# Turning one block of attention probabilities by two transposing transfers instead of on TensorE

## The chip, the cores and the metric

The kernel runs on one core of a Trainium2 chip. The metric is the device time of one execution in microseconds (us). The kernel before took 906.15 us, the median of three runs (905.28 to 908.67).

## What is computed

An encoder trunk of two layers on 256 tokens with 1024 features, in float32. One projection of the normalised input gives the inputs of two branches and two gates; their sum goes through an output projection, a SwiGLU block and a per-layer embedding. The reference, cut to the part around the change:

```python
def hybrid_layer(h, ...):
    u = rms_norm(h, g_mix_pre)
    (gq, gk, gv, gg, ra_f, ra_b, aq, ak, av, gate_a, gate_b) = split(u @ w_in)
    o_gla = rms_norm(o_f + o_b, g_gla_out)          # gated linear attention, both directions
    branch_a = (o_gla * silu(gg)) @ w_o_gla
    q = rope(rms_norm(aq, g_q_norm)); k = rope(rms_norm(ak, g_k_norm))
    branch_b = gqa_attention(q, k, av) @ w_o_attn   # 8 heads in 2 groups, softmax over 256 keys
    mixed = sigmoid(gate_a) * branch_a + sigmoid(gate_b) * branch_b
    h = h + rms_norm(mixed @ w_out, g_mix_post)
    ...
```

## The kernel before

**Products.** Every float32 matrix product is made of three matmuls of fp32r operands: each operand is split into a high part (a cast, on ScalarE, ACT in the profile) and a low part (source minus high part, on VectorE, DVE); both are written by `split`, L135. A block of weights of 1 MB is loaded by SyncE's queue (SP, L298), split into `wh` and `wl`, and used by 24 matmuls of 128x512, 12 for each half of the tokens (8 with `wh`, 4 with `wl`, L123). The class `Stream` holds three raw buffers and four pairs of split weights, so a load starts when a raw buffer has been split, and a split starts when TensorE (PE) is done with an older pair. `ws.cast` is the pair of instructions, cast and subtraction, of the weight split made last.

**Order.** The program is written as a main line of weight products and a set of tasks. After each product a `tick()` counts the tasks down; a task whose count is up writes its next piece and yields the next count. A scheduler then sorts each engine's instructions by that order, with a few raised in priority (`tc.high_priority`) and a few tied behind another instruction (`tc.issue_after`). The result is one fixed order for each engine; at run time an engine takes its instructions in that order and waits at any whose inputs are not there.

**The stages that matter here**, in each of the two layers, by the part of the name behind the underscore and the layer's number: `v` and `gg` (the value and out-gate projections of the gated linear attention, GLA), `gla` (its scores and its four outputs, `outputs`, L1384 on), `at0`/`at1` (the softmax attention of the two groups of heads), `gate` (the product of gate A as plain blocks, that of gate B in a form with seven products of quarter blocks instead of eight, and the product of branch A with `w_o_gla`). What runs there:

- Attention, `attend(g)`, for the two query halves `hf` of group g: scores and `softmax` (exponentials at L1237 on ACT, normalising at L1244 on DVE) give a tile of probabilities `pr_`, 128 queries by 4 heads by 256 keys. `turn_p` (L1249 on) transposes it on PE, eight 128x128 blocks into two banks of PSUM (L1254), and splits each bank (L135, tiles `mid_0at`). Then 6 matmuls of 128x512 multiply by the values (`aux_0at`), and the result is split into `aT` (`big_0at`).
- The four GLA outputs: 12 matmuls of 128x256 each, two squares with their sums on ACT (L1396), the reciprocal root on GpSimd (POOL, L494 and L495), two scalings on DVE (L544), into the tile `on`, whose index s is the half of the tokens: the outputs come for half 0 twice, then for half 1 twice.
- The out-gate, `out_gate`, starts when the GLA and the attention tasks are both over: sigmoids on ACT (L1457), eight products on DVE (L128, tiles `mid_0gg`), then `turn_out`: the 16-bit halves of the words are set apart by an ACT copy (L466) and transposed by an SP transfer (L467), four in all; later `take_in` joins them again (ACT copy, L476) and splits them into `gT` (`big_0gg`), the operand of the branch-A product `m`.
- The sums that the seven-product form of gate B needs: `whole` (four additions at L1510, two products at L128, one split) and four more additions at L131, then splits into `mid_0gate`; between the weights, additions of whole weight blocks (L327, L330, L333, in `Stream.step`).

The string `GATES` gives the order of the weight products of the gate stage: three of gate A (u), then gate B (digits) and branch A (m) interleaved.

Of the kernel before, what the change touches and what calls it, by code (L numbers as in the profile page):

```python
# [11 lines left out]
F32R = mybir.dt.float32r  # L12
BF16 = mybir.dt.bfloat16
U16 = mybir.dt.uint16
# [4 lines left out]
P = 128  # L19
# [6 lines left out]
AHEAD, EMPTY, EMPTY_FIRST = 400, 100, 1600  # L26
# [5 lines left out]
WAIT_SPREAD = 12  # L32
W = dict(r=5, z=6, s0=4, s=3, s1=9, o0=1, o=1, k=4, q=3, a0=1, a1=4, a2=4, a3=1)
WAIT_GATED = 9, 11

STEPS_FIRST = "00 10 01 11 02 12 03 13".split()
STEPS = "00 01 02 10 03 11 12 13".split()
# [24 lines left out]
def trunk_kernel(ctx: ExitStack, tc: tile.TileContext, a: dict, out: bass.AP):  # L62
# [7 lines left out]
    nc = tc.nc  # L70
# [13 lines left out]
    def nm(s):  # L84
        uid[0] += 1
        return f"{s}_{part[0]}_{uid[0]}"

    def big(dt=F32):
        return bigp.tile([P, 2048], dt, tag="big", name=nm("big"))

    def mid(dt=F32):
        return b4p.tile([P, 1024], dt, tag="mid", name=nm("mid"))
# [4 lines left out]
    def aux():  # L97
        return accp.tile([P, 512], F32, tag="acc", name=nm("aux"))
# [16 lines left out]
    def passes(o, parts, start, stop, fresh=False, between=None, **kw):  # L115

        ps = [((xh, yh), (xh, yl), (xl, yh)) if fresh else ((xh, yh), (xl, yh), (xh, yl)) for (xh, xl), (yh, yl) in parts]  # L120
        seq = [p for t in ps for p in t[:2]] + [t[2] for t in ps]
        for n, (x, y) in enumerate(seq):
            nc.tensor.matmul(o, x, y, start=start and n == 0, stop=stop and n == len(seq) - 1, **kw)  # L123
            if between is not None and 2 * (n + 1) == len(seq):
                between()
# [7 lines left out]
    def split(hi, lo, src):  # L133

        return nc.scalar.copy(hi, src), nc.vector.tensor_tensor(out=lo, in0=src, in1=hi.bitcast(F32), op=ALU.subtract)  # L135


    h = cp.tile([P, 2, D], F32, tag="h", name="h")
# [229 lines left out]
    ws = Stream(4)  # L368
# [101 lines left out]
    def take_in(hi, lo, src, parts, behind=()):  # L470

        tn = hi.shape[-1]
        with ExitStack() as order:
            for x in behind:
                order.enter_context(tc.issue_after(x.ins))
            nc.scalar.copy(  # L476
                parts.bitcast(U16).rearrange("p (k t s) -> p k t s", s=2, t=tn),
                src.bitcast(U16).rearrange("p (s k t) -> p k t s", s=2, t=tn),
            )
            split(hi, lo, parts.rearrange("p (k t) -> p k t", t=tn))  # L480
# [65 lines left out]
    def halves(t):  # L546
        return [t[:, j * 512 : (j + 1) * 512] for j in range(2)]
# [501 lines left out]
    for l in range(DEPTH):  # L1049
# [199 lines left out]
        def turn_p(pr_):  # L1249
            res = []  # L1250
            for s in range(2):
                ps = aux()
                for i in range(4):
                    nc.tensor.transpose(ps[:, i * P : (i + 1) * P], pr_[:, i, s * P : (s + 1) * P], ident)  # L1254
                pT = halves(mid(F32R))
                split(pT[0], pT[1], ps)
                res.append(pT)
            return res

        def attend(g):  # L1260
            qs = []
            for hf in range(2):
                yield W["q"]
                ps = aux()
                for i in range(4):
                    hd = 4 * g + i
                    nc.tensor.transpose(ps[:, i * P : (i + 1) * P], qrs[hf][:, hd * P : (hd + 1) * P], ident)
                qh, ql = halves(mid(F32R))
                split(qh, ql, ps)
                qs.append((qh, ql, qss[hf][:, 4 * g : 4 * g + 4]))  # L1270
            keys.need()
            yield W["a0"]
            prs = []
            for hf in range(2):
                prs.append(softmax(g, hf, qs[hf]))
                yield W["a1"]
            for hf in range(2):
                pT = turn_p(prs[hf])
                yield W["a2"]
                o = aux()  # L1280
                vs = [slice(s * 256 + g * P, s * 256 + (g + 1) * P) for s in range(2)]
                passes(o, [((avh[:, c], avl[:, c]), pT[s]) for s, c in enumerate(vs)], True, True)
                aT.put(o, 4 * g, 4, hf * P, P)
                yield W["a3"]

        def attention():
            for g_ in range(2):
                part[0] = f"{l}at{g_}"
                yield from attend(g_)
# [90 lines left out]
        on = big().rearrange("p (s c) -> p s c", s=2)  # L1380
# [70 lines left out]
        def out_gate():  # L1451
            while not (gla.over and attention.over):
                yield 1
            for hf in range(2):
# [11 lines left out]
                def turn(hf=hf, xs=xs):  # L1466
                    for j, x in enumerate(xs):
                        yield WAIT_GATED[hf] if j == 0 else 1
                        take_in(*gT.at(4 * j, 4, hf * P, P), *x)
# [322 lines left out]
```

## Time and profile before

| | before |
|---|---|
| median of 3 runs | 906.15 us |
| the profiled execution | 905.28 us, of it 903.5 us from its first to its last instruction |
| granted TensorE clock | 0.998 of full speed |
| PE busy | 894.6 us (99%), 4447 matmuls |
| DVE busy | 790.9 us (88%) |
| ACT busy | 634.5 us (70%) |
| POOL busy | 105.4 us (12%) |
| HBM read | 169.50 MB |

The times in the profile are microseconds from the start of the span. A row of the timeline gives the start, the time up to the end of the last of the row's instructions, the engine, line, operation, output tile and inputs, their shapes and how many instructions the row stands for; brackets at its end give idle time before it and what ended it. A tile `mid_0at` is one of the pool `mid`, layer 0, stage `at`. A row of the windows gives, for a stretch of time, the busy us (and number of instructions) of PE, PE's weight loads, DVE, ACT and POOL, then the clock, the share of the transfer engines and their GB/s.

### The profile page before, as it was taken

To read this page: it belongs to the slowest core of one execution; us is meant where nothing else is said; L and a number is where in the kernel's file an instruction comes from. 1 tells how busy PE (TensorE), PEld (TensorE's weight loads), DVE (VectorE), ACT (ScalarE), POOL (GpSimd) and SP (SyncE) were. 2 spreads that over 40 slices of the span, in tenths; PEclk is the share of its full clock that TensorE was granted. 3 is DMA by queue.
4 is the path that set the end of the run, shared out by engine and by line. 5 is a ranking of instruction groups with operands and counts; after the bars stand their busy time and mean duration, and the time that the engine had idled before them with its cause. 6 is when DMAs were issued, how large, how long until landed. Compare 5 with 4: busy or idle time off the path is not lost.

```text
span 903.5 us, 12157 instructions
## 1 busy us (share of the span) xinstructions
PE 894.6 (99%) x4447; PEld 759.9 (84%) x4447; DVE 790.9 (88%) x1021; ACT 634.5 (70%) x1027; POOL 105.4 (12%) x157
## 2 busy tenths in 40 slices
PE   9999999999999999999999999999999999999996
PEld 8888888878888888888898888888888888888886
DVE  7899979988569989999779799799985799999984
ACT  7678769856468787766676687698645697867653
POOL 3800111220110000000334001210001100000001
PEclk9999999999999999999999999999999999999999
DMA  8764448369296785947476424475672966857441
GB/s 285 255 200 138 140 140 236 138 231 315 66 328 192 208 266 175 291 171 265 161 268 213 160 94 140 140 232 184 218 251 91 306 187 221 255 182 261 151 176 47
DMA packets 116967, 180.25 MB, mean 200 GB/s; under 512 B 30942, under 2 KB 55014, under 8 KB 116396
## 3 DMA queue, kind: packets, MB, share of 16 engines
q1 hardware_dynamic: 116748, 179.35, 60.9%
q8 instruction: 35, 0.57, 0.3%
q14 instruction: 24, 0.20, 0.1%
q10 hardware_dynamic: 160, 0.14, 0.0%
HBM read 169.50 MB, written 3.15 MB: 191 GB/s over the span
## 4 chain that ended last, share of the span: by engine, by line
PE 86%; DVE 6%; ACT 3%; issue 3%; POOL 1%; DMA 1%; POOLq 0%; ACTq 0%; DVEq 0%
PE acc_0ffnin L123 12%; PE acc_1ffnin L123 11%; PE acc_1gate L123 7%; PE acc_1ffnin L107 7%; PE acc_0ffnin L107 7%; PE acc_1rq L123 3%; PE acc_1gqk L107 2%; PE acc_0wout L123 2%; PE acc_0ple L123 2%; PE acc_1gg L123 2%; PE acc_1v L123 2%; PE acc_0v L123 2%; PE acc_1merge L123 2%; PE acc_0merge L123 2%; PE acc_1ple L123 2%
## 5 line engine op out<-in xcount | busy, mean ns | idle before, releaser
L135 ACT CAST wh_1ffnin<-raw_1ffnin 128x1024 fp32r<-128x1024 f32 x38 | 38.7, 1051 | 20.8 <-PE acc_1ffnin L107 11.1
L135 ACT CAST wh_0ffnin<-raw_0ffnin 128x1024 fp32r<-128x1024 f32 x38 | 38.5, 1049 | 19.4 <-PE acc_0ffnin L107 9.3
L135 DVE TENSOR_TENSOR wl_0ffnin<-raw_0ffnin,wh_0ffnin 128x1024 fp32r<-128x1024 f32 x38 | 44.9, 1221 | 4.0 <-ACT wh_0ffnin L135 4.0
L135 DVE TENSOR_TENSOR wl_1ffnin<-raw_1ffnin,wh_1ffnin 128x1024 fp32r<-128x1024 f32 x38 | 45.0, 1221 | 2.8 <-ACT wh_1ffnin L135 2.7
L107 PE MATMUL acc_0ffnin<-wh_0ffnin,big_0ffnin 128*128 128x512 f32 x176 | 45.1, 390 | 0.0
L107 PE MATMUL acc_1ffnin<-wh_1ffnin,big_1ffnin 128*128 128x512 f32 x176 | 45.1, 390 | 0.0
L123 PE MATMUL acc_1ffnin<-wh_1ffnin,big_1wout 128*128 128x512 f32 x168 | 41.5, 389 | 0.0
L123 PE MATMUL acc_0ffnin<-wh_0ffnin,big_0wout 128*128 128x512 f32 x168 | 41.5, 389 | 0.0
L107 PEld LDWEIGHTS acc_0ffnin<-wh_0ffnin,big_0ffnin 128*128 128x128 f32 x176 | 33.0, 188 | 6.9
L107 PEld LDWEIGHTS acc_1ffnin<-wh_1ffnin,big_1ffnin 128*128 128x128 f32 x176 | 33.0, 188 | 6.9
L123 PEld LDWEIGHTS acc_1ffnin<-wh_1ffnin,big_1wout 128*128 128x128 f32 x168 | 31.5, 188 | 6.5
L123 PEld LDWEIGHTS acc_0ffnin<-wh_0ffnin,big_0wout 128*128 128x128 f32 x168 | 31.5, 188 | 6.5
L135 DVE TENSOR_TENSOR wl_1ffnin<-lent_1ffnin,wh_1ffnin 128x1024 fp32r<-128x1024 f32 x30 | 35.6, 1220 | 0.8 <-ACT wh_1ffnin L135 0.7
L135 DVE TENSOR_TENSOR wl_0ffnin<-lent_0ffnin,wh_0ffnin 128x1024 fp32r<-128x1024 f32 x30 | 35.7, 1220 | 0.3 <-ACT wh_0ffnin L135 0.3
L135 ACT CAST wh_1ffnin<-lent_1ffnin 128x1024 fp32r<-128x1024 f32 x30 | 30.5, 1054 | 5.4 <-PE acc_1ffnin L107 2.5
L135 ACT CAST wh_0ffnin<-lent_0ffnin 128x1024 fp32r<-128x1024 f32 x30 | 30.4, 1051 | 4.9 <-DVE wl_0ffnin L135 2.5
L135 DVE TENSOR_TENSOR wl_0gate<-raw_0gate,wh_0gate 128x1024 fp32r<-128x1024 f32 x20 | 24.7, 1265 | 3.2 <-ACT wh_0gate L135 3.1
L135 ACT CAST wh_0gate<-raw_0gate 128x1024 fp32r<-128x1024 f32 x20 | 20.2, 1055 | 7.4 <-PE acc_0gate L123 3.5
L135 DVE TENSOR_TENSOR wl_1gate<-raw_1gate,wh_1gate 128x1024 fp32r<-128x1024 f32 x20 | 23.6, 1220 | 1.6 <-ACT wh_1gate L135 1.6
L135 ACT CAST wh_1gate<-raw_1gate 128x1024 fp32r<-128x1024 f32 x20 | 20.1, 1046 | 6.4 <-PE acc_1gate L123 3.5
L107 PE MATMUL acc_1ffnin<-wl_1ffnin,big_1ffnin 128*128 128x512 f32 x88 | 24.1, 391 | 0.0
L107 PE MATMUL acc_0ffnin<-wl_0ffnin,big_0ffnin 128*128 128x512 f32 x88 | 24.0, 391 | 0.0
(730 smaller groups left out, 2745.1 us busy)
## 6 DMA issues: line engine op xcount, KB each, us to landing
raw_0ffnin<-in_w_ffn_out_dram SPq DMA_DIRECT2D x11, 1024.0 KB, 5.2
raw_1ffnin<-in_w_ffn_out_dram SPq DMA_DIRECT2D x11, 1024.0 KB, 5.9
lent_0ffnin<-in_w_ffn_in_dram SPq DMA_DIRECT2D x6, 1024.0 KB, 5.1
lent_1ffnin<-in_w_ffn_in_dram SPq DMA_DIRECT2D x6, 1024.0 KB, 6.9
raw_0v<-in_w_in_dram SPq DMA_DIRECT2D x4, 1024.0 KB, 5.2
raw_0gate<-in_w_o_gla_dram SPq DMA_DIRECT2D x4, 1024.0 KB, 5.3
raw_0gate<-in_w_o_attn_dram SPq DMA_DIRECT2D x4, 1024.0 KB
raw_0wout<-in_w_ffn_in_dram SPq DMA_DIRECT2D x8, 512.0 KB, 4.6
```

Of the source, the lines that this page charges most:

```text
L107: return nc.tensor.matmul(o, lhsT, rhs, start=start, stop=stop)
L123: nc.tensor.matmul(o, x, y, start=start and n == 0, stop=stop and n == len(seq) - 1, **kw)
L135: return nc.scalar.copy(hi, src), nc.vector.tensor_tensor(out=lo, in0=src, in1=hi.bitcast(F32), op=ALU.subtract)
```

## The change

For group 1 and the first query half, in each layer, the eight PE transposes are replaced. `turn_p_out` sets the two 16-bit planes of each half of the keys apart by an ACT copy into `on[:, 1, :]`, which is still free, and one SP transfer for each half transposes them back into the tile of the probabilities. After three more ticks `turn_p_in` joins the planes by an ACT copy into `on[:, 1, :]`, tied behind the last weight split written so far, and splits the result from there. The second query half still goes through `turn_p`.

```diff
+TURNED_P, WAIT_P = (0,), 3
...
+        def turn_p_out(pr_, hf):
+            flat, planes = pr_.rearrange("p h k -> p (h k)"), on[:, 1 - hf, :]
+            with tc.high_priority(AHEAD):
+                for s, t in enumerate(halves(planes)):
+                    nc.scalar.copy(
+                        t.bitcast(U16).rearrange("p (z h f) -> p z h f", z=2, f=P),
+                        pr_[:, :, s * P : (s + 1) * P].bitcast(U16).rearrange("p h (f z) -> p z h f", z=2),
+                    )
+            xs = list(zip(halves(flat), halves(planes)))
+            for src, t in xs:
+                nc.sync.dma_start_transpose(out=src.bitcast(U16).rearrange("p (x t) -> p x t", t=P), in_=t.bitcast(U16))
+            return xs
+
+        def turn_p_in(xs):
+            res = []
+            for src, t in xs:
+                pT = halves(mid(F32R))
+                take_in(*(x.rearrange("p (k t) -> p k t", t=P) for x in pT), src, t, ws.cast)
+                res.append(pT)
+            return res
...
             for hf in range(2):
                 prs.append(softmax(g, hf, qs[hf]))
                 yield W["a1"]
+                if g and hf in TURNED_P:
+                    prs[hf] = turn_p_out(prs[hf], hf)
             for hf in range(2):
-                pT = turn_p(prs[hf])
+                if g and hf in TURNED_P:
+                    yield WAIT_P
+                    pT = turn_p_in(prs[hf])
+                else:
+                    pT = turn_p(prs[hf])
                 yield W["a2"]
```

Lines behind the new functions move by 28 (L1510 becomes L1538), those ahead by 1. The attention task of group 1 now ends later, by which more moves than the probabilities. On PE, besides the eight transposes that go, the second half's eight transposes move from ahead of the first GLA output to behind the third, and its six value products from inside the first gate product to behind two gate products. GpSimd's order stays as it was, and SP gets the two transfers between two weight loads. Three places of the fixed order follow, of layer 0; layer 1 has the same.

The first is DVE around the last GLA outputs (`aux_0gla_..`; the scaled outputs go into `big_0gla_..929`, which is `on`). Before, from an addition of `whole` just ahead of the first output's scaling to the scaling of the third:

```order
L1510 TENSOR_TENSOR mid_0gate_250_1615<-big_start_46_303 128x512
L544 SCALAR_TENSOR_TENSOR big_0gla_136_929<-aux_0gla_237_1492,hss_0gla_238_1493,ggla_0gla_135_927 128x256 x2
L1510 TENSOR_TENSOR mid_0gate_251_1616<-big_start_22_149 128x512
L1510 TENSOR_TENSOR mid_0gate_251_1616<-big_start_46_303 128x512
L128 TENSOR_TENSOR mid_0gate_251_1616<-mid_0gate_251_1616,rope0_0kv_91_638 128x512 x2
L544 SCALAR_TENSOR_TENSOR big_0gla_136_929<-aux_0gla_239_1518,hss_0gla_240_1519,ggla_0gla_135_927 128x256 x2
L135 TENSOR_TENSOR mid_0gate_252_1623<-mid_0gate_251_1616,mid_0gate_252_1623 128x512
L131 TENSOR_TENSOR mid_0gate_251_1616<-mid_0gate_251_1616 128x512
L131 TENSOR_TENSOR t512_0gate_253_1626<-mid_0gate_250_1615,mid_0gate_251_1616 128x512
L131 TENSOR_TENSOR mid_0gate_251_1616<-mid_0gate_251_1616,mid_0gate_250_1615 128x512
L131 TENSOR_TENSOR mid_0gate_250_1615<-mid_0gate_250_1615,t512_0gate_253_1626 128x512
L544 SCALAR_TENSOR_TENSOR big_0gla_136_929<-aux_0gla_241_1544,hss_0gla_242_1545,ggla_0gla_135_927 128x256 x2
```

In the changed kernel, on DVE from the scaling of the last output on:

```order
L545 SCALAR_TENSOR_TENSOR big_0gla_136_929<-aux_0gla_241_1566,hss_0gla_242_1567,ggla_0gla_135_927 128x256 x2
L1538 TENSOR_TENSOR mid_0gate_247_1602<-big_start_22_149 128x512
L1538 TENSOR_TENSOR mid_0gate_247_1602<-big_start_46_303 128x512
L1538 TENSOR_TENSOR mid_0gate_248_1603<-big_start_22_149 128x512
L1538 TENSOR_TENSOR mid_0gate_248_1603<-big_start_46_303 128x512
L129 TENSOR_TENSOR mid_0gate_248_1603<-mid_0gate_248_1603,rope0_0kv_91_638 128x512 x2
L136 TENSOR_TENSOR mid_0gate_249_1610<-mid_0gate_248_1603,mid_0gate_249_1610 128x512
L136 TENSOR_TENSOR big_0at_234_1521<-aux_0at_253_1642,big_0at_234_1521 128x4x128
L132 TENSOR_TENSOR mid_0gate_248_1603<-mid_0gate_248_1603 128x512
L132 TENSOR_TENSOR t512_0gate_250_1613<-mid_0gate_247_1602,mid_0gate_248_1603 128x512
L132 TENSOR_TENSOR mid_0gate_248_1603<-mid_0gate_248_1603,mid_0gate_247_1602 128x512
L132 TENSOR_TENSOR mid_0gate_247_1602<-mid_0gate_247_1602,t512_0gate_250_1613 128x512
```

Before, the additions of `whole` and the sums stood between the scalings; now all of them stand behind the last scaling, behind the split `big_0at_..1521` of the second half's value product too.

The second place is DVE a few rows on: the out-gate's products (`mid_0gg`) and the splits of the weights `wl_0gate_..1665` (gate B's first), `..1722` (gate A's last) and `..1756` (gate B's second), which were `..1689`, `..1726` and `..1768`. Before, from the split of the last attention result to the first addition of weights:

```order
L135 TENSOR_TENSOR big_0at_230_1461<-aux_0at_249_1606,big_0at_230_1461 128x4x128
L128 TENSOR_TENSOR mid_0gg_254_1636<-mid_0gg_254_1636,big_0gg_201_1276 128x512 x2
L128 TENSOR_TENSOR mid_0gg_254_1636<-mid_0gg_254_1636,big_0gla_136_929 128x512 x2
L128 TENSOR_TENSOR mid_0gg_255_1646<-mid_0gg_255_1646,big_0gg_201_1276 128x512 x2
L128 TENSOR_TENSOR mid_0gg_255_1646<-mid_0gg_255_1646,big_0gla_136_929 128x512 x2
L135 TENSOR_TENSOR mid_0gate_256_1657<-mid_0gate_250_1615,mid_0gate_256_1657 128x512
L135 TENSOR_TENSOR mid_0gate_257_1666<-mid_0gate_251_1616,mid_0gate_257_1666 128x512
L135 TENSOR_TENSOR mid_0gate_258_1675<-mid_0gate_251_1616,mid_0gate_258_1675 128x512
L135 TENSOR_TENSOR wl_0gate_265_1689<-lent_0gate_259_1678,wh_0gate_264_1688 128x1024 x2
L135 TENSOR_TENSOR mid_0gate_266_1701<-t512_0gate_253_1626,mid_0gate_266_1701 128x512
L327 TENSOR_TENSOR lent_0gate_259_1678<-lent_0gate_259_1678,lent_0gate_261_1682 128x2048
```

In the changed kernel, from the split of gate B's first weights to that of its second:

```order
L136 TENSOR_TENSOR wl_0gate_261_1665<-lent_0gate_255_1654,wh_0gate_260_1664 128x1024 x2
L136 TENSOR_TENSOR mid_0gate_251_1624<-mid_0gate_247_1602,mid_0gate_251_1624 128x512
L136 TENSOR_TENSOR mid_0gate_252_1633<-mid_0gate_248_1603,mid_0gate_252_1633 128x512
L136 TENSOR_TENSOR mid_0gate_254_1651<-mid_0gate_248_1603,mid_0gate_254_1651 128x512
L328 TENSOR_TENSOR lent_0gate_255_1654<-lent_0gate_255_1654,lent_0gate_257_1658 128x2048
L129 TENSOR_TENSOR mid_0gg_262_1677<-mid_0gg_262_1677,big_0gg_201_1276 128x512 x2
L129 TENSOR_TENSOR mid_0gg_262_1677<-mid_0gg_262_1677,big_0gla_136_929 128x512 x2
L129 TENSOR_TENSOR mid_0gg_263_1687<-mid_0gg_263_1687,big_0gg_201_1276 128x512 x2
L129 TENSOR_TENSOR mid_0gg_263_1687<-mid_0gg_263_1687,big_0gla_136_929 128x512 x2
L136 TENSOR_TENSOR mid_0gate_264_1697<-t512_0gate_250_1613,mid_0gate_264_1697 128x512
L136 TENSOR_TENSOR wl_0gate_267_1722<-raw_0gate_258_1660,wh_0gate_266_1721 128x1024 x2
L136 TENSOR_TENSOR wl_0gate_272_1756<-big_0gate_256_1656,wh_0gate_271_1755 128x1024 x2
```

Before, the eight out-gate products stood ahead of the first gate-B split; now they stand behind it and behind the first addition of weights, and the split of gate A's last weights stands behind all of these.

The third place is PE, where gate A's last block uses that split (`acc_..1729` and `1730` now, `1733` and `1734` before, are its two halves of the tokens). Before:

```order
L123 MATMUL acc_0gate_279_1776<-wh_0gate_264_1688,big_start_22_149 128x512 x8
L123 MATMUL acc_0gate_279_1776<-wl_0gate_265_1689,big_start_22_149 128x512 x4
L123 MATMUL acc_0gate_271_1733<-wh_0gate_268_1725,big_start_46_303 128x512 x8
L123 MATMUL acc_0gate_271_1733<-wl_0gate_269_1726,big_start_46_303 128x512 x4
L123 MATMUL acc_0gate_272_1734<-wh_0gate_268_1725,big_start_46_303 128x512 x8
L123 MATMUL acc_0gate_272_1734<-wl_0gate_269_1726,big_start_46_303 128x512 x4
```

In the changed kernel:

```order
L124 MATMUL acc_0gate_275_1764<-wh_0gate_260_1664,big_start_22_149 128x512 x8
L124 MATMUL acc_0gate_275_1764<-wl_0gate_261_1665,big_start_22_149 128x512 x4
L124 MATMUL acc_0gate_269_1729<-wh_0gate_266_1721,big_start_46_303 128x512 x8
L124 MATMUL acc_0gate_270_1730<-wh_0gate_266_1721,big_start_46_303 128x512 x7
L124 MATMUL acc_0gate_269_1729<-wl_0gate_267_1722,big_start_46_303 128x512 x2
L124 MATMUL acc_0gate_270_1730<-wh_0gate_266_1721,big_start_46_303 128x512
L124 MATMUL acc_0gate_270_1730<-wl_0gate_267_1722,big_start_46_303 128x512 x2
```

Before, each half's matmuls with `wh` were followed by its own with `wl`; now seven of the second half's `wh` matmuls are taken ahead of the first that needs `wl_0gate_..1722`.

## The prediction

> **What bounds the kernel now.** First the page: what is busy, and the chain that ended last.
>
> ```profile
> span 903.5 us, 12157 instructions
> ...
> PE 894.6 (99%) x4447; PEld 759.9 (84%) x4447; DVE 790.9 (88%) x1021; ACT 634.5 (70%) x1027; POOL 105.4 (12%) x157
> ...
> PE 86%; DVE 6%; ACT 3%; issue 3%; POOL 1%; DMA 1%; POOLq 0%; ACTq 0%; DVEq 0%
> ```
>
> PE is the bound. Next, what PE waits for in the whole span:
>
> ```profile
> PE warm L107 <- POOL seed L144: 1.0, 1, 1.0
> PE aux_1wout L450 <- DVE mid_1wout L544: 0.4, 1, 0.4
> PE acc_0gqk L107 <- DVE mid_0at L135: 0.2, 1, 0.2
> ```
>
> Nothing, 1.6 us in all. So a step taken from PE gains just its time there, nothing else can gain, and any lateness elsewhere that reaches PE is lost for good, since PE has no idle time to make it up in. What matters is how near the other engines are to being late. The windows around the change, two of layer 0 and one of layer 1:
>
> ```profile
> 126.00:140.00 14.00, 14.00 (x90) 12.60 (x89) 11.05 (x21) 9.44 (x24) 5.02 (x8) 1.00 0.38 111
> 140.00:164.00 24.00, 24.00 (x108) 19.87 (x107) 24.00 (x30) 21.99 (x30) 0.53 (x1) 1.00 0.88 249
> ...
> 591.00:615.00 24.00, 24.00 (x107) 19.88 (x106) 24.00 (x29) 21.98 (x30) 0.43 (x1) 1.00 0.80 241
> ```
>
> DVE, the third number of busy time, has 3 us free from 126 to 140 (the GLA outputs) and not a moment from 140 to 164 (the gate stage), in layer 1 likewise. There PE is fed by a DVE that works without a pause. That is the place to watch.
>
> **What goes from PE.** The timeline of PE: the transposes of the first half with the row behind them, the later value products, the last GLA output, and the gate stage.
>
> ```profile
> 115.69 1.03 PE L1254 MATMUL aux_0at<-ident,mid_0at 128*128 128x128 f32 x8
> 116.48 1.63 PE L123 MATMUL acc_0gg<-wh_0v,big_start 128*128 128x512 f32 x6
> ...
> 123.41 1.52 PE L123 MATMUL aux_0at<-mid_0at,big_0kv 128*128 128x512 f32 x6
> ...
> 135.47 1.60 PE L107 MATMUL aux_0gla<-v_0v,big_0gla 128*128 128x256 f32 x12
> 136.90 1.55 PE L123 MATMUL acc_0gate<-wh_0gg,big_start 128*128 128x512 f32 x6
> ...
> 157.33 1.98 PE L123 MATMUL acc_0gate<-wh_0gate,big_start 128*128 128x512 f32 x8
> 159.14 1.07 PE L123 MATMUL acc_0gate<-wl_0gate,big_start 128*128 128x512 f32 x4
> ...
> 162.77 1.98 PE L123 MATMUL acc_0gate<-wh_0gate,mid_0gate 128*128 128x512 f32 x8
> ...
> 165.49 1.98 PE L123 MATMUL acc_0gate<-wh_0gate,big_0gg 128*128 128x512 f32 x8
> ```
>
> Matmuls overlap, so a step costs the distance between starts: eight transposes 116.48 - 115.69 = **0.79 us**, eight matmuls of 128x512 159.14 - 157.33 = 1.81 (0.227 each), a GLA output 136.90 - 135.47 = 1.43. The change takes 0.79 per layer from PE; the rest of its work there only changes places.
>
> The Trainium skill ("VectorE: DVE Perf Modes", sections "The three transpose paths" and "Rules for kernel authors") gives 390 ns for a 128x128 bf16 transpose on TensorE and 1309 ns by the transfers' crossbar, and says to use TensorE where PSUM will do, which speaks against this change. By its figure 16 blocks of two bytes would take 20.9 us (an estimate), and the value products would wait. This trace differs on both: 0.79 us for eight float32 blocks on PE, and the landing times below for eight two-byte blocks.
>
> **What the new path costs.** The rows around the place (the end of the normalising on DVE, a weight load on SP, ACT's idle times), and the same kinds of steps at the out-gate, which uses the same path for its four pieces:
>
> ```profile
> 108.41 0.61 DVE L1244 TENSOR_SCALAR mid_0at<-mid_0at,sm_0at 128x256 f32<-128x256 f32 x2
> ...
> 113.31 0.37 SPq L298 DMA_DIRECT2D raw_0gg<-in_w_in_dram  x1
> ```
>
> ```profile
> 111.04 0.57 ACT L1237 ACTIVATE mid_0at<-aux_0at,mx_0at,qss_0rq 128x256 f32<-128x256 f32 x1 [1.74 <-DVE mx_0at L1231]
> ...
> 118.09 1.06 ACT L135 CAST mid_0at<-aux_0at 128x512 fp32r<-128x512 f32 x2
> ...
> 121.60 0.41 ACT L135 CAST big_0gla<-t_0gla 128x256 fp32r<-128x256 f32 x1 [1.11 <-DVE t_0gla L1376]
> ```
>
> ```profile
> L466 ACT COPY big_0gg<-mid_0gg x4: 1037/1042/1046, 145.9 to 149.7; 128x1024 uint16<-128x1024 uint16 x4
> ```
>
> ```profile
> L476 ACT COPY big_0gg<-mid_0gg x4: 1173/1178/1189, 155.2 to 161.3; 128x1024 uint16<-128x1024 uint16 x4
> ```
>
> ```profile
> L467 SPq DMA_TRANSPOSE mid_0gg<-big_0gg x4: 1257/1334/2047, 147.0 to 152.0; - x4
> ...
> DMA to landing us min/median/max: 3.2/4.1/4.1
> ```
>
> Two copies and two joins add at most 2 x 1.04 + 2 x 1.18 = 4.4 us to ACT per layer. The copies start when the probabilities are normalised (108.41 + 0.61, and ACT's casts ahead), about 109.2, and fall into the 1.74 us in which ACT waited ahead of 111.04; the tail of 0.3 us moves the second half's exponentials, whose transposes now come much later. The transfers issue at about 110.2 and 111.6 and land 4.1 us later, at 114.5 and 115.8 (estimates). In ACT's order the first join stands behind a weight cast and a gg evacuation, and so about where the two casts began that it replaces (118.09), at 117.9 by my layout: 2 us of slack. Joins, casts and subtractions are done by 124.1. The value products, at 123.41 before, now stand behind two outputs and three runs of six matmuls: 123.41 - 0.79 + 2 x 1.43 + 3 x 1.36 = 129.6, 5.5 us of slack. ACT's 1.11 us ahead of 121.60 takes most of the joins. The casts and subtractions read SBUF instead of PSUM; I take the 128x512 rows as they are. The tie behind the last weight cast costs nothing: that cast stands in the same order ahead of the join. The next weight load on SP stands behind the transfers, which have left SP by 112.9 (111.6 + 1.3); that load went at 113.31. So this part is hidden, and PE enters the gate stage 0.79 us earlier, with the last output done at 136.90 - 0.79 = 136.1.
>
> **What the later end of the attention moves.** As the order shows, the sums for gate B, which filled DVE's waits between the scalings, now stand behind the last scaling, and the out-gate's products behind them. The squares and the scalings, ACT and DVE:
>
> ```profile
> 129.28 0.20 ACT L1396 ACTIVATION_READ_ACCUMULATOR big_0gla<-aux_0gla 128x1 f32 x1
> ...
> 132.10 0.20 ACT L1396 ACTIVATION_READ_ACCUMULATOR big_0gla<-aux_0gla 128x1 f32 x1
> ```
>
> ```profile
> 130.66 0.88 DVE L544 SCALAR_TENSOR_TENSOR big_0gla<-aux_0gla,hss_0gla,ggla_0gla 128x256 f32<-128x256 f32 x2 [1.38 <-POOL hss_0gla L495]
> 131.45 1.29 DVE L1510 TENSOR_TENSOR mid_0gate<-big_start 128x512 f32<-128x512 f32 x2
> 132.66 1.29 DVE L128 TENSOR_TENSOR mid_0gate<-mid_0gate,rope_0kv 128x512 f32<-128x512 f32 x2
> 134.54 0.88 DVE L544 SCALAR_TENSOR_TENSOR big_0gla<-aux_0gla,hss_0gla,ggla_0gla 128x256 f32<-128x256 f32 x2 [0.59 <-POOL hss_0gla L495]
> ...
> 143.97 1.29 DVE L128 TENSOR_TENSOR mid_0gg<-mid_0gg,big_0gg 128x512 f32<-128x512 f32 x2
> ...
> 148.79 1.89 DVE L135 TENSOR_TENSOR mid_0gate<-mid_0gate,mid_0gate 128x512 fp32r<-128x512 f32 x3
> 150.59 2.36 DVE L135 TENSOR_TENSOR wl_0gate<-lent_0gate,wh_0gate 128x1024 fp32r<-128x1024 f32 x2
> 152.86 0.69 DVE L135 TENSOR_TENSOR mid_0gate<-t_0gate,mid_0gate 128x512 fp32r<-128x512 f32 x1
> 153.47 2.29 DVE L327 TENSOR_TENSOR lent_0gate<-lent_0gate,lent_0gate 128x2048 f32<-128x2048 f32 x1
> 155.67 2.36 DVE L135 TENSOR_TENSOR wl_0gate<-raw_0gate,wh_0gate 128x1024 fp32r<-128x1024 f32 x2
> ```
>
> From the last square to the scaling POOL took 130.66 - 129.48 = 1.2 us (134.54 - 132.30 = 2.2 in its slower form). The last squares, behind casts and evacuations on ACT, end at about 137.8, so the last scaling starts at 139.0. From there DVE's new order, by distances between starts: scaling 0.8, four additions 2.4, two products 1.2, the split of `mid_..1610` with its wait for the cast 1.2, attention split 0.6, four sums 2.5 (0.6 each), gate B's first weights 2.3, three operand splits 1.8, weight addition 2.2, eight out-gate products 148.79 - 143.97 = 4.8, a split 0.6, half of gate A's last weights 1.2: in all 21.6, so 160.6 to 160.9. PE wants that half at 157.33 - 0.79 plus fifteen `wh` matmuls of 3.4 = 159.9. **First stall, 1.0.**
>
> Then DVE goes on: other half 162.0, gate B's second weights 164.2, addition 166.4, first split of the branch-A operand 167.0. PE has done its products by 165.8: **second stall, 1.2.** Behind that stand one weight split (2.3) and, after one more operand split, the operand's second part at 170.6, wanted after eight and two matmuls at 169.7: **third stall, 0.9**; and about **0.4** at the split for gate B's fourth product. Sum 3.5; less the 0.79 that PE was ahead, **+2.7 us per layer**, 5.4 in both. Against the profiled execution of 905.28 this gives 910.7; the median of the runs is 0.87 above it, so **911.5**.
>
> The bounds of the unknown: the DVE chain would cost nothing if the scheduler's new order met all its needs (-0.79 per layer remains); with POOL's slower form at the last output, +1.05 per layer on top; and if ACT is as late again at the squares, 4.9 per layer.
>
> **The rivals.** (1) *DVE's late chain doesn't reach PE.* For it: PE's order takes seven `wh` matmuls ahead and so was made for later splits; there were 3 us of DVE idle. Against: those 3 us were idle between the scalings, where the sums no longer stand, and the next 24 us have none. It gives 905.28 - 1.6 = 903.7, with the median's 0.87 904.6. (2) *DVE is later still*, POOL's slower form or ACT's casts ahead of the last squares: +3.8 to 4.9 per layer, 913.7 to 916.0. (3) *The transfers land late.* From 6.3 us after issue, against 4.1 in the rows, the first join holds ACT and shifts its weight casts one for one; at 8 us that is 1.7 per layer on top, 915. Against it: in its place nothing is heavier than at the out-gate, whose landings had 249 GB/s beside them. (4) *The transfer works block by block.* If each of the 16 blocks took the 1.3 us that a transfer took on SP, the second half would land 21 us after 110.2, at 131; ACT would stand at the joins from 117.9 to 131, and its weight casts, 13 us late, would cost PE some 11 per layer beyond the slack of 2: about 928. The rows' 4.1 us for eight blocks speak against it. The Trainium skill's figure above would give this. (5) *The change gains more than its transposes*, over 0.5%: PE's waits of 1.6 us in all leave nothing to gain; it would need 4.5 us.
>
> **How the numbers follow.** My forecast 0.55 (its own range 908.5 to 913.7), (1) 0.17, (2) 0.20, (3) 0.05, (4) 0.01, (5) 0.02. About 0.5% is what a measurement of this kernel can tell from no change, so the limits are 901.6 and 910.7. The forecast, 911.5, lies just above; a bit over six tenths of its chance, 0.34, is slower. With (2), (3) and (4) slower has 0.60; same has (1) and the rest of the forecast, 0.38; faster 0.02. The range, 904.3 to 916.0, takes in (1) and the ends of (2).
>
> **What would show it.** PE's waits should list DVE at `wl_0gate` and `big_0gg` in the gate stage, about 3.5 us per layer, none at the value products; the sums should run behind 139 in one row with the scaling; the stretch to the start of the gate stage should be 0.8 us shorter. If the joins are what PE or ACT waits for, (3) was right; if PE shows no waits and the gate stage is as long as before, (1).

## The result and the profile after

The changed kernel took **910.82 us** (median of 6 runs, 910.17 to 912.35), the kernel before beside it 906.59 (6 runs, 905.28 to 908.67): ratio **1.0053**, 95% interval 1.0041 to 1.0064. It is slower, by 3.7 to 5.8 us; the forecast was 911.5. The profiled execution took 910.38 us against 905.28. The page of the changed kernel:

```profile
span 908.6 us, 12147 instructions
...
PE 894.8 (98%) x4431; PEld 756.9 (83%) x4431; DVE 791.2 (87%) x1021; ACT 642.4 (71%) x1035; POOL 100.7 (11%) x157
...
PE 80%; DVE 10%; ACT 4%; issue 3%; DMA 2%; POOL 1%; SPq 0%; POOLq 0%; ACTq 0%; DVEq 0%
```

16 matmul instructions are gone, and yet the span is 5.1 us longer. In the chain that ended last, DVE has 10% where it had 6%: at some places PE now waits for it. Which, the list of PE's waits says (engine, tile and line waiting, what it waited for, us in total, times, longest):

```profile
PE acc_1gate L124 <- DVE big_1gg L136: 1.4, 2, 0.9
PE acc_0gate L124 <- DVE big_0gg L136: 1.3, 2, 0.9
PE acc_0gate L124 <- DVE wl_0gate L136: 1.2, 2, 0.8
...
PE acc_1gate L124 <- DVE wl_1gate L136: 0.8, 1, 0.8
```

The rows left out are the three that the kernel before had. All new rows are of the gate stage, and all name DVE: the splits of weights (`wl`) and of the branch-A operand (`big_gg`). None names the value products, a transfer or a join. The windows of layer 0:

```profile
126.00:140.00 14.00, 14.00 (x84) 12.40 (x83) 8.03 (x14) 7.22 (x21) 3.85 (x8) 1.00 0.43 150
140.00:164.00 24.00, 23.19 (x103) 18.80 (x102) 23.27 (x32) 20.46 (x26) 0.00 (x0) 1.00 0.61 180
```

DVE did 11.05 us of work between 126 and 140 before and does 8.03 now, 3 us less, while its total is the same (790.9 and 791.2). What moved is more than these 3 us: the eleven operations of `whole` and the sums, 6.7 us by the distances between their starts, ran from 126.67 to 138.7 before and run from 139.46 to 147.6 now, while a weight split and the last scaling came ahead of 140 in exchange. They now stand in a stretch in which DVE had no room. Three rows of DVE show it, the last scaling of a GLA output and what follows at once, and the split that PE waits for first:

```profile
138.67 0.87 DVE L545 SCALAR_TENSOR_TENSOR big_0gla<-aux_0gla,hss_0gla,ggla_0gla 128x256 f32<-128x256 f32 x2
139.46 2.49 DVE L1538 TENSOR_TENSOR mid_0gate<-big_start 128x512 f32<-128x512 f32 x4
...
159.27 2.36 DVE L136 TENSOR_TENSOR wl_0gate<-raw_0gate,wh_0gate 128x1024 fp32r<-128x1024 f32 x2
```

And PE there, with its waits in brackets:

```profile
135.75 2.00 PE L124 MATMUL acc_0gate<-wh_0gg,big_start 128*128 128x512 f32 x8
...
156.18 3.56 PE L124 MATMUL acc_0gate<-wh_0gate,big_start 128*128 128x512 f32 x15
160.55 0.73 PE L124 MATMUL acc_0gate<-wl_0gate,big_start 128*128 128x512 f32 x2 [0.81 <-DVE wl_0gate L136]
...
162.75 1.99 PE L124 MATMUL acc_0gate<-wh_0gate,mid_0gate 128*128 128x512 f32 x8
...
166.76 1.90 PE L124 MATMUL acc_0gate<-wh_0gate,big_0gg 128*128 128x512 f32 x7 [0.90 <-DVE big_0gg L136]
...
170.24 1.89 PE L124 MATMUL acc_0gate<-wh_0gate,big_0gg 128*128 128x512 f32 x7 [0.41 <-DVE big_0gg L136]
...
172.87 1.98 PE L124 MATMUL acc_0gate<-wh_0gate,mid_0gate 128*128 128x512 f32 x8
...
178.17 0.73 PE L124 MATMUL acc_0gate<-wl_0gate,mid_0gate 128*128 128x512 f32 x2 [0.38 <-DVE wl_0gate L136]
...
184.82 1.98 PE L124 MATMUL acc_0gate<-wh_0gate,mid_0gate 128*128 128x512 f32 x8
```

Four waits in layer 0, at the four places that were forecast; layer 1 has the first three of them (614.26, 620.47 and 623.95), and no wait at the fourth.

What each part of a layer gained and lost is read from PE's rows at which a stage starts. Of the kernel before, the merge stage of layer 0, then the gg, gate and merge stages of layer 1:

```profile
201.43 1.98 PE L123 MATMUL acc_0merge<-wh_0gate,big_0at 128*128 128x512 f32 x8
...
552.86 2.00 PE L123 MATMUL acc_1gg<-wh_1v,big_0ple 128*128 128x512 f32 x8
...
587.78 1.55 PE L123 MATMUL acc_1gate<-wh_1gg,big_0ple 128*128 128x512 f32 x6
...
651.73 1.98 PE L123 MATMUL acc_1merge<-wh_1gate,big_1at 128*128 128x512 f32 x8
```

The same of the changed kernel:

```profile
204.22 1.98 PE L124 MATMUL acc_0merge<-wh_0gate,big_0at 128*128 128x512 f32 x8
...
555.47 2.00 PE L124 MATMUL acc_1gg<-wh_1v,big_0ple 128*128 128x512 f32 x8
...
589.47 2.00 PE L124 MATMUL acc_1gate<-wh_1gg,big_0ple 128*128 128x512 f32 x8
...
656.53 1.98 PE L124 MATMUL acc_1merge<-wh_1gate,big_1at 128*128 128x512 f32 x8
```

From gg to gate, layer 1: 34.92 before, 34.00 now, 0.92 us gained. From gate to merge: 63.95 before, 67.06 now, 3.11 lost. In layer 0 the gate stage took 201.43 - 136.90 = 64.53 before and 204.22 - 135.75 = 68.47 now, 3.94 lost; from gg (101.96 before, 101.75 now) to gate 0.94 was gained. So the layers are 3.0 and 2.2 us longer, 5.2 together; the spans differ by 5.1.

### The profile page after: what moved, and what is told of

Read it like the earlier page. It is cut to its first block, busy times and chain, and to the rows that moved or that the text cites. A ratio compares the mean times of both kernels' runs of the same rounds, so it can differ in the third digit from the quotient of the medians.

```text
span 908.6 us, 12147 instructions
## 1 busy us (share of the span) xinstructions
PE 894.8 (98%) x4431; PEld 756.9 (83%) x4431; DVE 791.2 (87%) x1021; ACT 642.4 (71%) x1035; POOL 100.7 (11%) x157
## 4 chain that ended last, share of the span: by engine, by line
PE 80%; DVE 10%; ACT 4%; issue 3%; DMA 2%; POOL 1%; SPq 0%; POOLq 0%; ACTq 0%; DVEq 0%
PE acc_0ffnin L124 12%; PE acc_1ffnin L124 11%; PE acc_0ffnin L108 7%; PE acc_1ffnin L108 7%; PE acc_1gate L124 4%; PE acc_1rq L124 3%; PE acc_1gqk L108 2%; PE acc_0wout L124 2%; PE acc_0ple L124 2%; PE acc_1v L124 2%; PE acc_0v L124 2%; PE acc_1merge L124 2%; PE acc_0merge L124 2%; PE acc_1gg L124 2%; PE acc_0gg L124 2%
## 5 line engine op out<-in xcount | busy, mean ns | idle before, releaser
L136 ACT CAST wh_1ffnin<-raw_1ffnin 128x1024 fp32r<-128x1024 f32 x38 | 38.6, 1050 | 19.9 <-PE acc_1ffnin L108 10.0
L136 ACT CAST wh_0ffnin<-raw_0ffnin 128x1024 fp32r<-128x1024 f32 x38 | 38.6, 1050 | 19.7 <-PE acc_0ffnin L108 10.0
L136 DVE TENSOR_TENSOR wl_0ffnin<-raw_0ffnin,wh_0ffnin 128x1024 fp32r<-128x1024 f32 x38 | 44.9, 1219 | 2.7 <-ACT wh_0ffnin L136 2.5
L136 DVE TENSOR_TENSOR wl_1ffnin<-raw_1ffnin,wh_1ffnin 128x1024 fp32r<-128x1024 f32 x38 | 45.0, 1220 | 2.3 <-ACT wh_1ffnin L136 2.2
L136 DVE TENSOR_TENSOR wl_1ffnin<-lent_1ffnin,wh_1ffnin 128x1024 fp32r<-128x1024 f32 x30 | 35.7, 1219 | 0.8 <-ACT wh_1ffnin L136 0.8
L136 DVE TENSOR_TENSOR wl_0ffnin<-lent_0ffnin,wh_0ffnin 128x1024 fp32r<-128x1024 f32 x30 | 35.7, 1220 | 0.5 <-ACT wh_0ffnin L136 0.5
L136 ACT CAST wh_1ffnin<-lent_1ffnin 128x1024 fp32r<-128x1024 f32 x30 | 30.4, 1050 | 6.1 <-DMA lent_1ffnin<-in_w_ffn_in_dram 2.7
L136 ACT CAST wh_0ffnin<-lent_0ffnin 128x1024 fp32r<-128x1024 f32 x30 | 30.4, 1051 | 5.4 <-DVE wl_0ffnin L136 2.5
L136 ACT CAST wh_0gate<-raw_0gate 128x1024 fp32r<-128x1024 f32 x20 | 20.2, 1052 | 10.1 <-DMA raw_0gate<-in_w_o_gla_dram 4.0
L136 ACT CAST wh_1gate<-raw_1gate 128x1024 fp32r<-128x1024 f32 x20 | 20.2, 1048 | 9.0 <-PE acc_1gate L124 4.1
L136 DVE TENSOR_TENSOR wl_0gate<-raw_0gate,wh_0gate 128x1024 fp32r<-128x1024 f32 x20 | 24.0, 1243 | 1.0 <-ACT wh_0gate L136 1.0
L136 DVE TENSOR_TENSOR wl_1gate<-raw_1gate,wh_1gate 128x1024 fp32r<-128x1024 f32 x20 | 23.5, 1218 | 0.8 <-ACT wh_1gate L136 0.7
```

## The experiments

Theory A was that the loss comes from the order: the attention ends later, the sums for gate B slip behind the last scaling, and DVE is late for the whole gate stage. Its rival, theory B, was that the new path itself costs the time: copies and joins on ACT, transfers on SP's queue. A ratio is to the kernel before on the same chip. Diffs are against the changed kernel, unless said otherwise.

### The pause alone

The first half stays on PE; only the pause of three products ahead of it is kept. DVE's order from the last scalings on is that of the changed kernel.

```diff
-                if g and hf in TURNED_P:
-                    prs[hf] = turn_p_out(prs[hf], hf)
...
                 if g and hf in TURNED_P:
                     yield WAIT_P
-                    pT = turn_p_in(prs[hf])
-                else:
-                    pT = turn_p(prs[hf])
+                pT = turn_p(prs[hf])
```

> The first half's transposes stay on TensorE, only the pause of three products ahead of them is kept; no transfers, no extra ACT copies. Theory A (the loss comes from the later end of the attention, which puts the sums for gate B behind the last GLA scaling): the waits of the gate stage are all there and the 0.79 us per layer of transposes is back, so 912.4 us, ratio 1.0064 (1.005 to 1.008). Theory B (the loss comes from the copies, transfers and joins): as before, ratio 0.999 to 1.002, and no wait of TensorE in the gate stage.

Measured: 912.21 us, ratio **1.0071** (1.0058 to 1.0083). PE's waits in its gate stages:

```profile
PE acc_0gate L124 <- DVE big_0gg L136: 1.4, 2, 0.9
PE acc_1gate L124 <- DVE big_1gg L136: 1.4, 2, 0.9
...
PE acc_0gate L124 <- DVE wl_0gate L136: 1.0, 2, 0.8
PE acc_1gate L124 <- DVE wl_1gate L136: 0.8, 1, 0.8
```

Without a transfer and without a join, the same waits stand at the same tiles with nearly the same lengths. The pause alone brings the whole loss. The transposes that stayed cost 0.0018 more than the change, 1.6 us as expected, though the two intervals overlap.

### The path alone

The copies, transfers and joins run, but between the two still unused halves of the tile `on`; nobody uses what they bring, and the attention goes its way as before.

```diff
-            xs = list(zip(halves(flat), halves(planes)))
+            xs = list(zip(halves(on[:, hf, :]), halves(planes)))
...
-                    prs[hf] = turn_p_out(prs[hf], hf)
+                    Task(turn_p_in(turn_p_out(prs[hf], hf)), part[0])
...
-                if g and hf in TURNED_P:
-                    yield WAIT_P
-                    pT = turn_p_in(prs[hf])
-                else:
-                    pT = turn_p(prs[hf])
+                pT = turn_p(prs[hf])
```

Here `turn_p_in` yields the pause itself and makes only the two joins, tied behind the last weight split as in the change.

> The copies, transfers and joins run beside the kernel before with nobody using what they bring (they go from and to the still unused halves of the tile of GLA outputs); the transposes stay on TensorE where they were, and so does the order. Theory A: the added 4.4 us per layer on ACT and the transfers are hidden, ratio 0.999 to 1.002. Theory B: ratio 1.005 or more, with waits of TensorE from ACT or the transfers.

Measured: 906.57 us, ratio **1.0003** (0.9994 to 1.0011). The path costs no time that can be told from none, at most about 1 us by the interval. Theory B falls for the loss as a whole. The run is harder on the path than the change is: its joins stand earlier in ACT's order (114.03 in layer 0, against 117.57 in the change), and ACT waits at the first join for its transfer, 0.23 us in layer 0 and 1.71 in layer 1. In the profiled execution, the slowest of the eleven with 908.59 us, PE has short waits for casts in the gate stages (`wh_0gate` 0.6 us, `wh_1gate` 0.2), and these stages took 64.96 and 64.53 us, 0.4 and 0.6 more than before. The one in layer 0 stands behind a load from memory that landed late, at a place where the kernel before waits too; what made ACT late in layer 1 wasn't traced.

### The second half's transposes ahead of the pause

```diff
+            kept = None
             for hf in range(2):
                 if g and hf in TURNED_P:
+                    kept = turn_p(prs[1])
                     yield WAIT_P
                     pT = turn_p_in(prs[hf])
                 else:
-                    pT = turn_p(prs[hf])
+                    pT = kept or turn_p(prs[hf])
```

> The changed kernel, but the second half's transposes are written ahead of the pause, so the sums for gate B stand between the scalings again; transfers and joins as in the change. Theory A: the loss goes and the gain of 0.79 us per layer stays, 904.5 to 906, ratio 0.998 to 0.9995. Theory B: the loss stays, ratio 1.004 or more.

Measured: **903.33** us, ratio **0.9968** (0.9957 to 0.9979): faster than the kernel before, and by more than was expected. PE's waits, the complete list:

```profile
PE warm L108 <- POOL seed L145: 1.0, 1, 1.0
PE aux_1wout L451 <- DVE mid_1wout L545: 0.7, 1, 0.7
PE acc_0gqk L108 <- DVE mid_0at L136: 0.2, 1, 0.2
```

DVE around the first scaling, where the sums (L1540 here) stand again:

```profile
126.38 1.28 DVE L1540 TENSOR_TENSOR mid_0gate<-big_start 128x512 f32<-128x512 f32 x2
128.61 0.88 DVE L545 SCALAR_TENSOR_TENSOR big_0gla<-aux_0gla,hss_0gla,ggla_0gla 128x256 f32<-128x256 f32 x2 [0.95 <-POOL hss_0gla L496]
```

The transfers and the joins are the same as in the change; only the order differs, and the waits of the gate stage are gone. PE's rows at five places of layer 0 (the gate stage's start, three products within it that the change has too, and the merge stage):

```profile
135.79 2.00 PE L124 MATMUL acc_0gate<-wh_0gg,big_start 128*128 128x512 f32 x8
...
161.66 1.98 PE L124 MATMUL acc_0gate<-wh_0gate,mid_0gate 128*128 128x512 f32 x8
...
169.82 1.98 PE L124 MATMUL acc_0gate<-wh_0gate,mid_0gate 128*128 128x512 f32 x8
...
180.70 1.98 PE L124 MATMUL acc_0gate<-wh_0gate,mid_0gate 128*128 128x512 f32 x8
...
199.74 1.98 PE L124 MATMUL acc_0merge<-wh_0gate,big_0at 128*128 128x512 f32 x8
```

This stage, 63.95 us, is the one without waits against which the change is measured: the change, which starts it 0.04 earlier, stands 1.13 us later at the first of the three products (162.75), 3.09 at the second (172.87), 4.16 at the third (184.82).

The same kernel, with the pause of three, was profiled a second time.

> The kernel with the second half's transposes ahead of the pause again, one look for a second profile: 902.5 to 904.5, from the gg stage to the gate stage 34.0 to 34.1 us in both layers, no wait of TensorE in the gate stage.

Measured: 903.54 us, the one run. From the gg stage to the gate stage it took 34.04 and 34.05 us, and no wait of PE stands in a gate stage, all as expected.

### The sums alone, early

Here the late attention stays as in the change, pause and all; only the call of `whole` moves, from the start of gate B to behind the first half's joins.

```diff
                     pT = turn_p_in(prs[hf])
+                    early.append(whole())
...
-        forms = sums(whole)
+        forms = sums(early[0])
```

> The changed kernel; the only edit is that the additions for gate B (whole) are written right behind the first half's joins instead of at the start of gate B. The second half's transposes, the pause and the end of the attention stay as late as in the change. Theory A, exact form (it is the sums standing behind the last scaling that make DVE late, not the late attention itself): the waits of the gate stage go, 904 to 906, ratio 0.997 to 1.000. Theory A2 (the late end of the attention is enough, since the out-gate's sigmoids, its transfers and the second value products stay late): ratio 1.003 or more with waits on big_gg.

Measured: **903.13** us, ratio **0.9967** (0.9954 to 0.9979). In this kernel the second half's transposes and value products are as late as in the change (133.30 and 141.07, against 133.45 and 141.22), and it is as fast as the kernel with the early transposes. Its two windows of layer 0:

```profile
126.00:140.00 14.00, 14.00 (x85) 12.36 (x84) 11.99 (x20) 10.31 (x24) 6.98 (x8) 1.00 0.44 148
140.00:164.00 24.00, 24.00 (x108) 19.88 (x107) 23.61 (x27) 22.99 (x29) 0.00 (x0) 1.00 0.90 228
```

DVE has its work ahead of 140 again (11.99 us against 8.03), and PE has no idle moment behind it. So the place of the sums is enough to take the loss away; that the attention ends late costs nothing that can be seen by itself.

How much of the gain is the sums' and how much the transposes', was told by the same move in the kernel before (the diff is against that one):

```diff
                 pT = turn_p(prs[hf])
+                if g and hf == 0:
+                    early.append(whole())
...
-        forms = sums(whole)
+        forms = sums(early[0])
```

> The kernel before (all transposes on TensorE), with only the additions for gate B written early, as in the run of the change with early sums. It tells what part of that run's gain (2.7 us) is the early sums alone and what the transposes. Theory A: the two transposing stages give 0.9 us per layer, so this is 1.8 us slower than that run, 904.9, ratio 0.998 to 1.000. If the early sums give it all: ratio 0.996 to 0.9975.

Measured: 904.83 us, ratio 0.9989 (0.9980 to 0.9998). The early sums alone give 0.0011 of the gain, and the turning by transfers the other 0.0022, 2.0 us for both layers (1.8 expected; the two intervals don't meet). The stretch from the gg stage to the gate stage says the same without any median: 33.99 to 34.06 us in every kernel here with the transfers in use, 34.92 to 34.94 in every one without, in both layers.

### A shorter pause, and another order

Three more kernels tried other ways to the same gain. None gained, and none came out at the ratio that was expected if its order was mended. The first has a pause of one product (`WAIT_P` 1 for 3):

> The changed kernel with a pause of one product instead of three. The sums for gate B stand between the scalings again. Theory A: no late chain in the gate stage; but the joins come about 5 us earlier in ACT's order, ahead of the landing by up to 2 us, so ACT waits there once per layer and delays a weight cast: ratio 0.998 to 1.002. Theory B: ratio 1.004 or more.

Measured: 914.66 us, ratio **1.0092** (1.0078 to 1.0106), the slowest of all, though most of `whole` stood between the scalings. The reason that was given ahead, joins 5 us earlier that wait for the landing, didn't come: the transfers went at 110.6 and 112.0, and the joins ran at 117.1, 0.4 earlier than in the change and without a wait. The longest of PE's waits in the gate stages:

```profile
PE acc_0gate L124 <- ACT wh_0gate L136: 3.3, 4, 1.6
PE acc_1gate L124 <- ACT wh_1gate L136: 2.2, 2, 1.6
```

Now it is ACT that is late. DVE behind the last scaling, which started at 139.71, and then ACT:

```profile
140.50 0.68 DVE L129 TENSOR_TENSOR mid_0gate<-mid_0gate,rope_0kv 128x512 f32<-128x512 f32 x1
```

```profile
145.72 0.62 ACT L136 CAST mid_0gate<-mid_0gate 128x512 fp32r<-128x512 f32 x1 [3.40 <-DVE mid_0gate L132]
146.36 1.28 ACT L1485 ACT_TABLE_LOAD   x1
```

One product of `whole` (L129) was left behind the last scaling, and with it the split and the four sums that need it; the cast of a sum on ACT waited for them, and in ACT's order the table load and the out-gate's sigmoids stand behind that cast, and the weight casts behind these.

The second kernel, with the pause of one as well, turns and multiplies the second half first:

```diff
-TURNED_P, WAIT_P = (0,), 3
+TURNED_P, WAIT_P = (0,), 1
...
-            for hf in range(2):
+            for hf in (1, 0) if g else (0, 1):
```

> The changed kernel, but the second half is turned on TensorE and multiplied first, and the joins of the first half come after it, one product later: the sums for gate B stand between the scalings again, and the transfers have more time to land. Theory A: ratio 0.996 to 0.999, as with the early transposes. What may go wrong is what went wrong with the pause of one: a single one of DVE's early operations left behind the last scaling makes ACT's weight casts late, then 1.003 or more with waits for wh_gate.

Measured: 910.27 us, ratio 1.0048 (1.0036 to 1.0061), the bad case that was named: here all of `whole` but its last split is done in time, and the four sums (L132) stand behind the last scaling on DVE. PE waits in layer 0 for `wh_0gate` (0.9 us) and for `wl_0gate` (1.1).

```profile
140.68 0.88 DVE L545 SCALAR_TENSOR_TENSOR big_0gla<-aux_0gla,hss_0gla,ggla_0gla 128x256 f32<-128x256 f32 x2 [0.87 <-POOL hss_0gla L496]
...
142.19 0.69 DVE L132 TENSOR_TENSOR mid_0gate<-mid_0gate 128x512 f32<-128x512 f32 x1
```

The third puts the pause of one and the early call of `whole` together (the two edits shown above):

> The changed kernel with a pause of one product and the additions for gate B written early. If the loss of the pause of one was again the sums for gate B behind the last scaling (this time holding up ACT: operand casts, table load, sigmoids, then the weight casts), it goes: ratio 0.996 to 0.999. If it was the joins or the transfers standing too early, it stays: 1.005 or more.

Measured: 907.97 us, ratio 1.0028 (1.0017 to 1.0039), between the two expectations: two thirds of the loss of the pause of one went. What is left stands again behind the last scaling (140.17), now a single sum on DVE:

```profile
140.96 0.68 DVE L132 TENSOR_TENSOR mid_0at<-mid_0at,t_0gate 128x512 f32<-128x512 f32 x1
```

ACT's cast, table load and sigmoids wait for it as in the first of the three. Over these three the loss falls with the work that stands there (one product, one split and four sums 1.0092; one split and four sums 1.0048; one sum 1.0028). That this work causes all of it is read from their rows and wasn't taken apart further. The amount alone is no measure: the change has all eleven operations there and lost less, 1.0053. In its order on ACT the first weight casts of gate B (144.19) stand ahead of the table load (146.20), in the kernel with the pause of one behind it (152.63 and 146.36).

## Why the prediction was right

The direction, the place, the engine and the size came out: 911.5 forecast, 910.82 measured, and for the profiled execution +5.4 forecast, +5.1 measured. The medians beside each other differ by less, 4.2 us, since the profiled execution of the kernel before was the fastest of its six. By its steps:

- **What goes from PE**: 0.79 us per layer was forecast, 0.94 and 0.92 gained. The transposes cost PE a little beside their own time: the six matmuls behind them took 1.47 us to the next row in the profile before (116.48 to 117.95), and the same six take 1.36 now (115.48 to 116.84).
- **The path is hidden**: right, bounded to about 1 us by the path alone and seen in the two kernels at 0.997, which have the path and no wait in a gate stage. The transfers went 0.8 us later than forecast (111.03) and landed later than the estimate, 4.5 to 5.0 us after issue against 4.1, which the slack took in: the first join started at 117.57 (117.9 was forecast), with no wait. ACT's busy time rose by 7.9 us, 4.0 per layer. Rivals (3) and (4) fall with this. The limit of 6.3 us in (3) was counted from the second transfer, but the first join needs only the first (in the path alone it started 4.9 us after the first went, 3.6 after the second), so it would have been 7.7. The Trainium skill ("VectorE: DVE Perf Modes", section "The three transpose paths") gives 1309 ns for a 128x128 block by the crossbar; sixteen blocks one after the other would need 21 us by it (an estimate). The trace has at most 5.0 us from issue to landing for eight blocks:

```profile
L1271 SPq DMA_TRANSPOSE mid_0at<-big_0gla x2: 1317/1330/1342, 111.0 to 112.4; - x2
...
DMA to landing us min/median/max: 4.5/4.7/5.0
```

- **The DVE chain**: the last scaling was forecast at 139.0 and started at 138.67; the split of gate A's last weights was to be half done at 160.6 to 160.9, and PE went on with it at 160.55.
- **The stalls**: by the distances from the kernel without waits, the first cost 1.13 us in layer 0 (1.0 forecast), the second and third together 1.96 (2.1), and the fourth 1.07, where 0.4 was forecast: the term most off. Its wait in the list of PE's matmuls is 0.38, but PE's weight loads (PEld) have a list of their own, and there PE's order takes two products in small pieces and waits for `wl_0gate` three times (0.80, 0.27 and 0.38). A fifth wait of the weight loads, 0.50 at 190.04, cost 0.36 more and wasn't forecast, so the stage lost 4.52. In layer 1 the first three places cost 3.07 and the fourth nothing, 3.11 in all. Together 7.6 us against 7.0 forecast; 1.9 against 1.6 was gained on PE; and the gate stage of layer 0 in the kernel before was itself 0.58 longer than without waits, which the sum didn't have. That these errors cancel to 5.2, near the 5.4, is luck; each place but the fourth is near its forecast without it.
- **Rival (1)**, that the late chain wouldn't reach PE, was wrong, though seven matmuls were taken ahead: they moved PE's need by 1.6 us, and DVE was later than that. **Rival (2)** didn't happen: POOL's slower form wasn't met at any of the eight outputs of both layers.
- **Rival (5)** was rightly held unlikely: the change didn't gain. The reason against it, that PE's 1.6 us of listed waits leave nothing else to gain, was not quite right: the list has the matmuls alone. The weight loads of the kernel before also waited in the gate stage of layer 0, behind a cast on ACT that waited for a load from memory:

```profile
PEld acc_0gate L123 <- ACT wh_0gate L135: 0.7, 2, 0.5
```

```profile
195.69 0.76 PEld L123 LDWEIGHTS acc_0gate<-wh_0gate,big_0gg 128*128 128x128 f32 x4 [0.54 <-ACT wh_0gate L135]
```

```profile
194.58 2.00 ACT L135 CAST wh_0gate<-raw_0gate 128x1024 fp32r<-128x1024 f32 x2 [1.11 <-DMA raw_0gate<-in_w_o_gla_dram]
```

That stage took 64.53 us, and 63.95 in both layers of the kernel before with the early sums, where these waits are gone: 0.58 of the 1.0 us that the early sums gave there. The other 0.4 can't be told from none (the interval is 0.2 to 1.8 us). The best kernels are 2.7 to 2.9 us under the one before, not the 4.5 of this rival.

## What to carry to other kernels

Where one engine is busy all the time and a second one nearly so, an edit that delays a task must be read in the order of all engines: what the fillers of the second engine's idle time are tied to, and whether they still stand ahead of the stretch where it has none. Here 6.7 us of DVE work, moved some 10 us later, cost 4.5 and 3.1 us in the next stage of the two layers, against the kernel without waits, while the path that the edit was about cost nothing that could be told. And what TensorE waits for must be read in both of its lists, that of the matmuls and that of the weight loads. Once seen, the loss is taken back by writing the filler early (or the step that it hangs on), and the edit then gives its gain: 903.1 to 903.3 us against 906.

## What had not been expected of the hardware

POOL's small operation ahead of a scaling (128x2) took 0.27 us at two outputs of layer 0 and 0.92 and 0.99 at the other two in the profile before. In the changed kernel all four of layer 0 took 0.27. These rows show the same step before and after:

```profile
132.40 0.99 POOL L494 TENSOR_SCALAR hss_0gla<-hss_0gla,em_start 128x2 f32<-128x2 f32 x1 [1.77 <-ACT big_0gla L1396]
```

```profile
129.02 0.27 POOL L495 TENSOR_SCALAR hss_0gla<-hss_0gla,em_start 128x2 f32<-128x2 f32 x1 [1.77 <-ACT big_0gla L1424]
```

In the first case DVE was at work on 128x512 additions and products (131.45 to 133.95), in the second it was idle, waiting for POOL until 130.10. So fillers on DVE seem to have a price on POOL: with the early sums one of these operations took 2.45 us (126.05 to 128.50), while DVE worked without a pause up to 128.37. In the kernel before, that with the early transposes and that with the early sums, the eight long ones of layer 0 (0.69 us or more) all ended 0.04 to 0.14 us behind the end of a DVE operation. Not every DVE operation goes with a long one: at 137.50 in the change it took 0.27 beside a subtraction that reads PSUM (L136, `aux_0at`). With the early sums POOL was busy for 6.98 us from 126 to 140, against 3.85 in the change, in the same eight instructions, and the kernel still gained. No run here tried this by itself, and times on POOL are rough in this profile.
